# A hybrid encoder trunk on one core: the depthwise convolution's operations given a later rank in the scheduler's order

## The chip, the cores and the metric

The kernel runs on one core of a Trainium2 chip. The core has five engines with a queue each: PE (matrix products; the trace lists its weight loads as PEld), DVE (vector work), ACT (activations, scaled copies), POOL (elementwise work in SBUF) and SP (which issues the DMAs here). Each works through its own queue in the order in which it was written, and semaphores hold an instruction until what it reads is there and what it overwrites is free. The metric is the device time of one execution in microseconds; lower is better.

## The reference

Two batches, a prompt of 512 rows and a sample of 1024 rows, go through the same layer with the same weights (width 1024, float32). Cut to what matters:

```python
h = _rmsnorm(x, norm_attn_g)
z = h @ w_in                     # q 512 | k 128 | v 128 | ca 512 | cb 512
a_out = _window_attn(q, k, v, bias, band, attn_sink)        # |q - k| <= 128
c = ca * jax.nn.sigmoid(cb)
c = _dwconv(c, conv_dw_w, conv_dw_b)                        # 31 taps, 512 channels
c = jax.nn.silu(_layernorm(c, conv_ln_g, conv_ln_b))        # over the channels
x = x + jnp.concatenate([a_out, c], axis=-1) @ w_out
h = _rmsnorm(x, norm_ffn_g)
u = _dwconv(h @ w_up, ffn_dw_w, ffn_dw_b)                   # 3 taps
x = x + (jax.nn.silu(u[..., :D_FF]) * u[..., D_FF:]) @ w_down
y = _rmsnorm(x, norm_final_g)
```

The change concerns the order of the 31-tap convolution `c = _dwconv(...)` among all else.

## The kernel before, in words

Every matrix product is made of three products of split operands (a high part and a rest), 128x128 stationary against 512 columns. The work runs in stages that overlap:

1. The prompt's projection (lines 487 to 501): `order` lists 14 chunks of 128 columns of `w_in`: four pairs `cb`, `ca` first, then `k`, `v` and four `q`. `want_raw` loads a chunk, `want_w` splits it (`split`: a cast on ACT, L189, and a subtraction on POOL, L190), `step` multiplies it (`proj`, L296, L297, L299) into a PSUM bank and `evac` takes it out: for `cb` a tanh on ACT (L360), for `ca` the gating on DVE (L369) into a padded input `cp` whose borders POOL clears (L365, L366), for `q` L373 and L374. Beside it the sample's rows are normed (`norm_in_place`, L242 to L247, with `rstd_of` on POOL, L173 and L174) and turned (`transposed`: L255 on PE, L257 on ACT, L258 on DVE).
2. The sample's projection, and beside it the prompt's attention (`scores`: L560 on PE, L567 on DVE; `values`: L616 to L642), its layer norm (`conv_norm`, L669 to L695) and its output projection (`out_half`, L711 to L716).
3. The prompt's feed-forward, 22 steps (`ffn_step`, with L837 and L841), and beside it the sample's attention.
4. The sample's layer norms and output projection, and then its feed-forward by a Strassen-like scheme (from 790 us on), where PE's order is written by hand.

The convolution itself is `conv_items(g, c, cp)`, one generator for each batch `g` (0 the prompt, 1 the sample) and group `c` of 128 channels. It works in pieces of 512 columns, one in the prompt and two in the sample. In each piece DVE accumulates most of the 31 taps in one PSUM bank (L335, then L339 for each further tap); the last `NOFF[g]` taps (4 in the prompt, 7 in the sample) are products on ACT (L328, L331) which POOL sums up in `pacc` (L332); at the end DVE adds the two (L347), and SP stores the piece to `cvd` in DRAM (L349). `conv_norm` loads it from there (L669), turns it on PE (L675), takes mean and variance on DVE (L677, L678), `rstd_of` on POOL, scales on DVE (L681) and turns back (L687).

Which instruction is traced where is set by hand: `tick()` runs three times within a projection and after each step and takes as many steps of the convolution's generators from the queues `convs` (prompt) and `late` (sample) as a credit allows. `drain(convs)` in `conv_norm` and `drain(late)` before the sample's first `conv_norm` trace what is left.

The order in which an engine then gets its instructions is not the traced one. The program is traced whole; each instruction gets a rank, a counter (`tc.cur_priority`) that goes up by one with each instruction traced; then a scheduler walks through a simulated time and gives each engine that is free, of the instructions that are ready, the one with the lowest rank. An instruction is ready when its inputs are there and the buffer that it writes has been released. Buffers are single ones with a fixed name: the kernel's `Slots` deals them out while the program is traced (15 `q` of 4096 bytes, 61 `h` of 2048, 4 `c`, 2 `d`), so that a tile's next user is fixed in traced order, whatever the ranks. The eight PSUM banks are `a` (3), `u` (2), `b` (2) and `c` (1, the convolution's accumulator).

The central lines:

```python
acc = bank("conv")
nc.vector.tensor_scalar(acc[:], src(0), w(0), cvb[:, c:c + 1], op0=ALU.mult, op1=ALU.add)
yield cost
for t in range(1, CK - noff):
    nc.vector.scalar_tensor_tensor(acc[:], src(t), w(t), acc[:], op0=ALU.mult, op1=ALU.add)
    if t % 2 == 1 and k < noff:
        offload(k)
```

Of the kernel before, what the change touches and what calls it, by code (L numbers as in the profile page):

```python
# [54 lines left out]
VG = 3  # L55
NW = 36
KEEP = 3
U0 = 2


# [82 lines left out]
def tile_hybrid_encoder(ctx: ExitStack, tc: tile.TileContext, xs, rel_bias, norm_attn_g, w_in,  # L143
# [9 lines left out]

    sb = Slots(big, dict(q=(15, 4096), c=(4, 4224), h=(61, 2048), d=(2, 2176), s=(32, 64)), "q", KEEP)
    banks = Slots(lambda tag: ps[two_of[tag]], dict(a=(3, 2048), u=(2, 2048), b=(2, 2048), c=(1, 2048)))
# [5 lines left out]
    def bank(job):  # L161
        return banks.tile([NT], among=use[job])
# [111 lines left out]
    def tick():  # L274
        pace["credit"] += pace["conv"] if convs else pace["late"]
        queue = convs or (late if pace["late"] else convs)
        while queue and pace["credit"] > 0:
            pace["credit"] -= advance(queue)
        if not queue:
            pace["credit"] = 0.0  # L280
        pace["due"] += pace["rate"]
        while side and pace["due"] >= 1.0:
            advance(side)
            pace["due"] -= 1.0
        if not side:
            pace["due"] = 0.0
# [5 lines left out]
    def proj(out, w, h, late_lo=False):  # L292
        whi, wlo = w
        for kc in range(KC):
            hi, lo = h[kc]
            nc.tensor.matmul(out, whi[:, kc, :], hi[:], start=(kc == 0), stop=False)  # L296
            nc.tensor.matmul(out, whi[:, kc, :], lo[:], start=False, stop=False)  # L297
            if not late_lo:
                nc.tensor.matmul(out, wlo[:, kc, :], hi[:], start=False, stop=(kc == KC - 1))  # L299
            if kc % 2 == 1 and kc < KC - 1:  # L300
                tick()
        for kc in range(KC if late_lo else 0):
            nc.tensor.matmul(out, wlo[:, kc, :], h[kc][0][:], start=False, stop=(kc == KC - 1))
# [8 lines left out]

    convs, late = deque(), deque()

    def conv_items(g, c, cp):
        T = GR[g]["T"]
        w = lambda t: cvw[:, t * 4 + c:t * 4 + c + 1]
        cost = 0.13 + NT / 960.0
        noff = NOFF[g]
        off = list(range(CK - noff, CK))  # L320
        for n in range(T // NT):
            src = lambda t: cp[:, t + n * NT:t + (n + 1) * NT]
            pacc = sb.tile([NT])

            def offload(k):
                t = off[k]
                if k == 0:
                    nc.scalar.activation(pacc[:], src(t), AF.Identity, scale=w(t))  # L328
                else:
                    pr = sb.tile([NT])  # L330
                    nc.scalar.activation(pr[:], src(t), AF.Identity, scale=w(t))  # L331
                    nc.gpsimd.tensor_tensor(pacc[:], pacc[:], pr[:], op=ALU.add)  # L332
# [4 lines that stand above are left out]
            k = 0  # L337
# [4 lines that stand above are left out]
                    k += 1  # L342
                yield cost
            while k < noff:
                offload(k)
                k += 1
            nc.vector.tensor_tensor(pacc[:], acc[:], pacc[:], op=ALU.add)  # L347
            del acc
            nc.sync.dma_start(cvd[g][:, c, n * NT:(n + 1) * NT], pacc[:])  # L349
            yield cost  # L350

    tanh_t, cpads, kt, vt = {}, {}, {}, {}
# [77 lines left out]
    def step(i, nt):  # L430
        kind, c, col = order[i]
        pp = bank("step")
        proj(pp[:], ws[i], h1[nt], i < 2 and nt == 0)
        evac(kind, c, nt, pp[:])
        if kind == "ca" and nt != 1:
            g = 0 if nt == 0 else 1
            (convs, late)[g].append(conv_items(g, c, cpads.pop((g, c))))
        tick()

    want_raw(1)  # L440
# [47 lines left out]
    for i in range(npr):  # L488
        if i == 3:
            side.append(make_h1(1))  # L490
        if i == 5:
            xq[2] = [load_x(GR[1], 4 + i) for i in range(4)]
            side.append(make_h1(2))
        if i == 1:
            constants()
            bbd = bias_to_dram()
        want_raw(i + 2)
        want_w(i + 1)
        step(i, 0)
        ws.pop(i)  # L500
# [299 lines left out]
    for i in range(npr, nch):  # L800
        want_raw(i + 2)
        want_w(i + 1)
        if i == nch - 1:
            for half in range(2):
                want_up_raw(0, half)
        for nt in range(1, 3):
            step(i, nt)
        ws.pop(i)
# [91 lines left out]
    def sample():  # L900
        sink_columns()
        yield from attention(8, 24)
        kt.clear(), vt.clear(), qt.clear(), bias.clear(), score_rows.clear()
        use.update(norm="a")
        pace.update(rate=RN)
        for m in range(16 + WOA):
            if m in (10, 12):
                load_cat(m // 2 - 1)
            if m < 16:
                load_wo(m // 2, m % 2)  # L910
            if m >= WOA:
                split_wo((m - WOA) // 2, m % 2, m % 4 < DW2)
                yield 0.0
        drain(late)
        for m in range(NE):
            yield from conv_norm(4 + m)

    pace.update(rate=RD, late=CD)
    for k in range(NJ):
        if k == U0:  # L920
            side.append(sample())
# [721 lines left out]
```

## Time and profile before

| | us |
|---|---|
| median of 3 runs | 1563.84 (1559.77 to 1566.2) |
| the profiled execution, its time | 1558.91 |
| the profiled execution, its span | 1557.1 |
| PE busy | 1506.9 |
| DVE busy | 1126.2 |
| ACT busy | 795.4 |
| POOL busy | 708.9 |

The profile is of one execution. A line of its timeline gives the start, the duration, engine and line of the kernel, the operation, the tile written and those read, and in brackets how long the engine stood idle before, and what ended that. A line of the waits gives who waited for whom, the sum, the number of times and the longest. A stage's row gives its length and, for each engine, the busy time and the number of instructions in it; PEclk is the share of PE's full clock that was granted. Idle time of an engine that isn't the bottleneck costs nothing.

### The profile page before, as it was taken

Reading aid. Unit: us, or ns where it says so; the run is one execution under the profiler, and the core shown is the slowest. Engines: PE = TensorE matmul, PEld = TensorE weight load, DVE = VectorE, ACT = ScalarE, POOL = GpSimd, SP = SyncE. Lnnn points to the kernel's source line nnn. Section 1 sums busy time; section 2 is a strip of 40 time slices with the busy share of each in tenths; the row PEclk is TensorE's granted clock in tenths of the full one; section 3 lists DMA queues with packets and bytes.
Section 4 is the critical chain, followed back from the end, with each engine's and each line's share of the span. In section 5 each row is a group of like instructions: output and inputs, shape, how many; then the busy total and the mean of one; then the engine's idle time right before and its main releaser. Section 6 shows DMA issues by size and latency. Waiting matters only on the chain. (4 is left out here: it accounts for less than half of the span.)

```text
span 1557.1 us, 20112 instructions
## 1 busy us (share of the span) xinstructions
PE 1506.9 (97%) x6843; PEld 1229.4 (79%) x6843; DVE 1126.2 (72%) x1604; ACT 795.4 (51%) x1404; POOL 708.9 (46%) x566
## 2 busy tenths in 40 slices
PE   8899998999999999899999999999999999999997
PEld 6787787787888888777777888888888788888885
DVE  7999767857788785344868777777776845568883
ACT  4634654335787786633454444455545543444254
POOL 7652344226666776947433455555554000003355
PEclk9999999999999999999999999999999999999999
DMA  7582334447343346779332233333331582356644
GB/s 230 156 212 81 107 100 124 129 142 217 112 132 129 118 129 181 242 238 298 114 93 76 92 104 104 105 104 102 102 115 64 200 284 82 105 165 230 221 135 162
DMA packets 228780, 227.17 MB, mean 146 GB/s; under 512 B 13268, under 2 KB 168348, under 8 KB 228549
## 3 DMA queue, kind: packets, MB, share of 16 engines
q1 hardware_dynamic: 228677, 225.88, 45.8%
q8 instruction: 54, 0.88, 0.2%
q14 instruction: 49, 0.40, 0.1%
HBM read 164.74 MB, written 62.14 MB: 146 GB/s over the span
## 5 line engine op out<-in xcount | busy, mean ns | idle before, releaser
L190 POOL TENSOR_TENSOR q<-q,q 128x1024 fp32r<-128x1024 f32 x72 | 173.4, 2415 | 93.4 <-ACT q L189 34.4
L940 POOL TENSOR_TENSOR q<-q,q 128x512 fp32r<-128x512 f32 x101 | 140.0, 1391 | 164.0 <-ACT q L1050 151.7
L940 DVE TENSOR_TENSOR h<-h,h 128x512 fp32r<-128x512 f32 (+2 forms) x202 | 153.9, 794 | 65.2 <-ACT h L944 25.3
L1398 PE MATMUL w<-h,h 128*128 128x512 f32 x462 | 181.4, 393 | 1.4 <-DVE q L1185 1.4
L1399 PE MATMUL w<-h,h 128*128 128x512 f32 x462 | 181.5, 393 | 0.0
L1400 PE MATMUL w<-h,h 128*128 128x512 f32 x462 | 181.1, 392 | 0.0
L1064 PE MATMUL w<-h,q 128*128 128x512 f32 x448 | 176.5, 394 | 1.0 <-ACT h L1147 0.6
L1066 PE MATMUL w<-h,q 128*128 128x512 f32 x448 | 175.5, 392 | 1.0 <-POOL q L940 1.0
L1065 PE MATMUL w<-h,q 128*128 128x512 f32 x426 | 166.4, 391 | 0.0
L296 PE MATMUL u<-h,q 128*128 128x512 f32 x400 | 161.0, 403 | 5.4 <-DVE h L837 4.1
L297 PE MATMUL u<-h,q 128*128 128x512 f32 x400 | 158.6, 397 | 0.0
L299 PE MATMUL u<-h,q 128*128 128x512 f32 x384 | 151.8, 395 | 2.7 <-POOL q L190 2.7
L937 POOL TENSOR_TENSOR q<-q,q 128x1024 f32<-128x1024 f32 x12 | 32.4, 2707 | 236.6 <-DVE q L937 220.0
L339 DVE SCALAR_TENSOR_TENSOR c<-c,cvw,c 128x512 f32<-128x512 f32 x184 | 138.0, 750 | 2.9
L944 ACT CAST h<-h 128x512 fp32r<-128x512 f32 x120 | 71.9, 619 | 93.2 <-DVE h L940 41.9
L296 PE MATMUL b<-h,q 128*128 128x512 f32 x256 | 102.7, 401 | 3.3 <-DVE d L369 2.2
L1398 PEld LDWEIGHTS w<-h,h 128*128 128x128 f32 x462 | 86.8, 188 | 21.6 <-ACT h L944 1.8
L1400 PEld LDWEIGHTS w<-h,h 128*128 128x128 f32 x462 | 86.7, 188 | 19.7
L1399 PEld LDWEIGHTS w<-h,h 128*128 128x128 f32 x462 | 86.8, 188 | 19.5
L837 DVE SCALAR_TENSOR_TENSOR h<-u,fw,h 128x511 f32<-128x511 f32 x88 | 65.5, 744 | 49.8 <-ACT h L841 49.0
L299 PE MATMUL b<-h,q 128*128 128x512 f32 x256 | 101.4, 396 | 0.0
L297 PE MATMUL b<-h,q 128*128 128x512 f32 x256 | 101.1, 395 | 0.0
(417 smaller groups left out, 3670.4 us busy)
## 6 DMA issues: line engine op xcount, KB each, us to landing
q<-in_w_up SPq DMA_DIRECT2D x88, 512.0 KB
ga<-q SPq DMA_DIRECT2D x64, 256.0 KB
h<-ga SPq DMA_DIRECT2D x57, 256.0 KB
q<-in_w_in SPq DMA_DIRECT2D x28, 512.0 KB
h<-in_w_down SPq DMA_DIRECT2D x52, 256.0 KB
q<-in_x_sample SPq DMA_DIRECT2D x15, 512.0 KB
h<-qsd SPq DMA_DIRECT2D x24, 256.0 KB
x1d<-q SPq DMA_DIRECT2D x11, 512.0 KB
```

The costliest lines, as they stand in the source:

```text
L190: (nc.vector if dve else nc.gpsimd).tensor_tensor(lo[:], raw[:], hi[:].bitcast(F32), op=ALU.subtract)
L296: nc.tensor.matmul(out, whi[:, kc, :], hi[:], start=(kc == 0), stop=False)
L297: nc.tensor.matmul(out, whi[:, kc, :], lo[:], start=False, stop=False)
L299: nc.tensor.matmul(out, wlo[:, kc, :], hi[:], start=False, stop=(kc == KC - 1))
L339: nc.vector.scalar_tensor_tensor(acc[:], src(t), w(t), acc[:], op0=ALU.mult, op1=ALU.add)
L940: (eng or nc.vector).tensor_tensor(out, a, b, op=ALU.subtract)
L1064: nc.tensor.matmul(out, whi[:, s], hi[:], start=(start and c == 0), stop=False, **go)
L1065: nc.tensor.matmul(out, whi[:, s], lo[:], start=False, stop=False, **go)
L1066: nc.tensor.matmul(out, wlo[:, s], hi[:], start=False, stop=(stop and c == 3), **go)
L1398: nc.tensor.matmul(out, sh[:, c], th[:], start=(p == 0), stop=False)
L1399: nc.tensor.matmul(out, sh[:, c], tl[:], start=False, stop=False)
L1400: nc.tensor.matmul(out, sl[:, c], th[:], start=False, stop=(p == NPAIR - 1))
```

## The change

The generator of each convolution is wrapped in another one, `behind`. Around each step it raises the rank counter by `n` and takes it back afterwards, so that whatever the step traces has a rank that is `n` higher: 200 in the prompt, 1500 in the sample. What is traced, where it is traced, the buffers and the paces stay as they are.

```diff
+BACK = (200, 1500)
...
     convs, late = deque(), deque()
+
+    def behind(gen, n):
+
+        while True:
+            tc.cur_priority += n
+            try:
+                cost = next(gen)
+            except StopIteration:
+                return
+            finally:
+                tc.cur_priority -= n
+            yield cost
...
         if kind == "ca" and nt != 1:
             g = 0 if nt == 0 else 1
-            (convs, late)[g].append(conv_items(g, c, cpads.pop((g, c))))
+            (convs, late)[g].append(behind(conv_items(g, c, cpads.pop((g, c))), BACK[g]))
```

## The prediction

> **What bounds the kernel now.** I read the page's busy line first, then the busy time by stage, then the waits of PE in the first stages, then the timeline around each wait.
>
> ```profile
> span 1557.1 us, 20112 instructions
> DVE  7999767857788785344868777777776845568883
> 40.00:181.00 141.00, 130.33 (x625) 106.07 (x624) 126.86 (x222) 74.62 (x147) 64.97 (x46) 0.99 0.50 139
> 181.00:260.00 79.00, 78.09 (x375) 63.90 (x374) 60.38 (x113) 43.55 (x93) 33.01 (x24) 1.00 0.44 118
> 260.00:280.00 20.00, 13.03 (x54) 10.47 (x53) 9.20 (x15) 8.55 (x17) 9.06 (x10) 0.74 0.40 125
> 280.00:640.00 360.00, 358.05 (x1698) 296.67 (x1698) 274.11 (x501) 236.09 (x436) 210.91 (x137) 1.00 0.48 147
> 640.00:800.00 160.00, 150.37 (x701) 121.26 (x700) 87.09 (x126) 61.74 (x117) 92.29 (x107) 0.98 0.61 200
> ```
>
> The columns of a stage are its length, then the busy time and count of PE, PEld, DVE, ACT and POOL, and PE's granted clock. PE carries the kernel: from 280 to 640 us it is idle for 360.00 - 358.05 = 1.95 us. It loses time in two places where the convolution also runs: 141.00 - 130.33 = 10.67 us between 40 and 181, and 6.97 us in the twenty microseconds from 260. In the first, DVE is itself busy 126.86 of 141 us (90%), and most of that is the prompt's convolution:
>
> ```profile
> 40.00:181.00 141.00, 78.29 (x104) 0.99 0.50 139
> 181.00:587.00 406.00, 138.00 (x184) 0.99 0.44 132
> ```
>
> This is the same view for line 339 alone, the taps on DVE: 78.29 of 126.86 us, 62%, in the prompt's stretch; in the sample's, 138.00 us spread over 406. So the question is how often a tap stands in front of something that PE waits for, and what a later convolution holds up in turn.
>
> **The change part by part.** Nothing is removed or added: the same instructions, tiles and DMAs, and the same buffers given out in the same order. What moves is the place of the convolution's instructions: in each of the prompt's four pieces 28 on DVE, 4 products on ACT, 3 sums on POOL and a store on SP, 144 in all, and in each of the sample's eight 25, 7, 6 and 1, 312 in all, within the order that the planner writes for each engine. By the counts of the stages above, PE, DVE, ACT and POOL together take 625+222+147+46 = 1040 instructions in 141 us, and 1698+501+436+137 = 2772 in 360: 7.4 and 7.7 per us. A rank 200 later is therefore about 27 us (estimate), one 1500 later about 195 us: in the prompt a step back, in the sample the end of every queue.
>
> *DVE in the prompt's stretch (gain).* The waits of PE from 40 to 181, but for one on ACT and one on a DMA:
>
> ```profile
> PE b L296 <- DVE d L369: 2.2, 1, 2.2
> PE u L616 <- DVE s L567: 2.0, 2, 1.1
> PE a L560 <- DVE s L567: 1.7, 1, 1.7
> PE u L299 <- POOL q L190: 1.2, 1, 1.2
> ...
> PE a L255 <- DVE h L258: 0.8, 1, 0.8
> PE a L631 <- DVE q L619: 0.6, 1, 0.6
> PE a L616 <- DVE s L583: 0.6, 1, 0.6
> ...
> PE b L296 <- DVE h L384: 0.4, 1, 0.4
> ```
>
> DVE ends 2.2+2.0+1.7+0.8+0.6+0.6+0.4 = 8.3 us of them. The two longest single ones in the timeline:
>
> ```profile
> 51.06 0.75 DVE L339 SCALAR_TENSOR_TENSOR c<-d,cvw,c 128x512 f32<-128x512 f32 x1
> 51.72 0.68 DVE L369 SCALAR_TENSOR_TENSOR d<-h,b 128x512 f32<-128x512 f32 x1
> 52.45 0.50 PE L296 MATMUL b<-h,q 128*128 128x512 f32 x1 [2.19 <-DVE d L369]
> ...
> 119.33 2.34 DVE L339 SCALAR_TENSOR_TENSOR c<-q,cvw,c 128x512 f32<-128x512 f32 x3
> 121.58 0.48 DVE L567 CUSTOM_DVE_ANT_0 h<-u,h,nsink 128x256 f32<-128x256 f32 x1
> 123.49 0.48 PE L560 MATMUL a<-h,h 128*128 128x256 f32 x2 [1.65 <-DVE s L567]
> ```
>
> A tap starts right before the evacuation (L369) that PE needs, and three run before the scores' evacuation (L567). A tap that ranks behind lets these go first, up to the one that is already running. The gain lies between 0 and 8.3 us; I take the taps' share of DVE's work, 62%, as the chance that the thing in front was a tap: **5.1 us**.
>
> *POOL around 265 (gain).*
>
> ```profile
> 268.60 1.26 POOL L332 TENSOR_TENSOR q<-q,q 128x512 f32<-128x512 f32 x1 [3.29 <-ACT q L331]
> 269.95 0.19 POOL L173 TENSOR_SCALAR s<-s 128x1 f32<-128x1 f32 x1
> 271.69 1.12 PE L687 MATMUL u<-ident,q 128*128 128x128 f32 x4 [4.03 <-DVE q L681]
> 276.61 1.09 PE L687 MATMUL u<-ident,h 128*128 128x128 f32 x4 [2.94 <-DVE h L681]
> ```
>
> PE stands 4.03 and 2.94 us for the prompt's last two layer norms. A sum of the sample's convolution (L332) runs 1.26 us on POOL just ahead of the first norm's variance (L173). Its rank falls by 1500, but POOL was idle when it became ready, and the planner doesn't hold a free engine back; so 0 to 1.3 us of the wait itself. The clock granted in that stage is 0.74: 13.03 us of work lose about 3.4 us by it, 10.4 with the idle time. I take the 1.3 and its share of the lost clock, 1.3/6.97 of 3.4: **1.9 us**; the bounds are minus and plus 10.4, since the order of this stage is written anew.
>
> [...]
>
> *The sample's convolution (nothing).* From 280 to 640 only 1.95 us of PE can be won. What a late end would cost depends on its first reader:
>
> ```profile
> 182.91 0.32 SPq L349 DMA_DIRECT2D cvd<-h  x1
> 194.24 0.58 SPq L669 DMA_DIRECT2D h<-cvd  x1
> ...
> 587.55 0.42 SPq L349 DMA_DIRECT2D cvd<-h  x1
> 663.22 0.57 SPq L669 DMA_DIRECT2D h<-cvd  x1
> 181.00:587.00 406.00, 396.17 (x1864) 326.79 (x1863) 315.01 (x568) 248.27 (x468) 216.13 (x148) 0.99 0.44 132
> ```
>
> The last piece of the sample is stored (L349) at 587.55 and read first (L669) at 663.22: 75.7 us of cover. All other DVE work in the 406 us is 315.01 - 138.00 = 177 us, 44%, so a tap that always goes last meets a free engine more than half the time: 0.75 us stretch to about 0.75/0.56 = 1.3, and a piece of 23 taps from 17 to 31 us, where the eight pieces now take 406/8 = 51 us each. The lag doesn't add up from piece to piece; I put the end 10 to 30 us later, inside the cover: 0. If the cover were gone, each microsecond past it would be one on PE's path. The prompt has less: stored at 182.91, read at 194.24, 11.3 us. Its taps can only lose what other work gains in front of them, 5 us by the term above; again 0, with up to 27 - 11.3 = 15.7 us of lateness if it lost all of its 200 ranks, which PE would fill with the sample's projections (the stage 181 to 260 has 78.09 of 79 us busy).
>
> *The buffers (nothing, with a bad upper end).* Each convolution tile is a single buffer whose next user was fixed in program order and waits for it, whatever its rank.
>
> ```profile
> 76.29 0.11 POOL L365 MEMSET d<- 128x15 f32 x1 [4.04 <-DVE c L339]
> 76.42 4.77 POOL L190 TENSOR_TENSOR q<-q,q 128x1024 fp32r<-128x1024 f32 x2
> ```
>
> The fourth prompt channel's input reuses the first one's buffer: POOL stood 4.04 us until the first channel's last tap, with two weight splits (L190) behind it. Postponing taps makes this later. PE has waited only 1.2 us for a split here (the L299 row above), so I take 0; the upper end is the first rival.
>
> *A rule against the change.* A tap accumulates in PSUM and keeps its time, while the norm's scaling (L247), which now goes first, does not:
>
> ```profile
> L339 DVE SCALAR_TENSOR_TENSOR c<-d,cvw,c x78: 740/756/757, 40.9 to 165.6; 128x512 f32<-128x512 f32 x78
> 50.39 0.75 DVE L247 TENSOR_SCALAR q<-q,s 128x1024 f32<-128x1024 f32 x1 [0.44 <-POOL s L174]
> 59.96 2.38 POOL L190 TENSOR_TENSOR q<-q,q 128x1024 fp32r<-128x1024 f32 x1
> 60.48 2.40 DVE L247 TENSOR_SCALAR q<-q,s 128x1024 f32<-128x1024 f32 x1
> ```
>
> L247 takes 0.75 us alone and 2.40 beside a split on POOL. The number of such meetings may go either way by a few, at 1.65 us of DVE each; I take none. [...]
>
> *Sum.* 5.1 + 1.9 = 7.0 us less. The profiled execution has a span of 1557.1 us and a time of 1558.91, 0.3% under the median of 1563.84. 1558.91 - 7.0 = 1551.9; against the median, times 1563.84/1558.91, **1557 us**.
>
> **The rivals.**
>
> *Slots in place of ranks (slower).* The convolution's tiles come free later, and what was given the same buffers waits: the memset above with the splits behind it, then in the sample the products and partial sums that sit in the half buffers of the weights (the q of the L332 row at 268.60 is such a half). For it: the 4.04 us on POOL, and that PE already waits 1.2 us for a split, so that the splits have no lead to spare there. Against: the planner sees these waits and fills an idle DVE with taps. Price: half of the 27 us of rank in the prompt, 13.5, and as much again from 181 to 280, where the weights are still split: 1558.91 + 27 = 1585.9, against the median about 1591; half of that, 1577, if only one of them bites. It decides from the point where the last tap of a piece moves by more than the lead of the split behind it.
>
> *The sample's convolution ends after its reader (slower).* If it really lost its 195 us of rank, it would end 195 - 75.7 = 119 us past the need, and PE would have little else: 1560 + 60 or more. Against: DVE's 56% of free time. Unlikely.
>
> *Nothing moves.* The taps already are what fills DVE: the planner gave evacuations with an earlier rank the way, and pieces end when the offloaded sums end, not the taps. A rank changes only ties; the step back isn't "behind all else" where nothing else is ready. 1558 to 1566 us.
>
> *The gain is eaten on DVE.* Four scalings (L247) or norms meet a split that they missed before: 4 x 1.65 = 6.6 us on an engine that is 90% busy, which leaves 0.4 of the 7.0: 1563 us. For it: the 2.40 above; against: as many may part.
>
> *Both holes close (much faster).* All of DVE's waits and the whole stage at 260: 8.3 + 10.4 = 18.7 us, 1540.2, against the median 1545.
>
> **How the numbers follow.** I tell no change from one within 0.5%, 7.8 us: faster is under 1556.0, slower over 1571.7. The forecast has a chance of 0.50 with its own range of 1549 to 1564, so near the bound that it gives 0.27 to faster and 0.23 to the same. Slots: 0.27, of it 0.25 slower. The late sample: 0.05, slower. Nothing moves: 0.05, the same. The gain eaten: 0.04, of it 0.03 the same, 0.01 slower. Both holes: 0.09, faster. Together faster 0.36, same 0.33, slower 0.31. The range leaves out the late sample and the tail of the slots above, and below it allows a little more than both holes: 1539 to 1592.
>
> **What would show it.** In the changed profile PE's waits between 40 and 181 that DVE ends fall from 8.3 to about 3 us; L369 and L567 no longer start right behind a tap. The stage from 260 (wherever the last norms then lie) keeps most of its hole. The last store of the sample's convolution lies between 597 and 618 us and no read of it waits; from 280 to 640 PE is idle 2 us or so. I am wrong if new waits of PE on POOL's L190 or on evacuations held up by a buffer appear between 60 and 280 (the slots), if PE waits for L669 after 640 (the late sample), or if the taps stand where they stood (nothing moves).

## The result: no change, and the profile after

The changed kernel takes 1562.26 us in the median of 12 runs (1558.83 to 1567.08); the kernel before, beside it, 1563.74 (1559.77 to 1571.06). The ratio is 0.9992, with a 95% interval of 0.9977 to 1.0007: no change. The forecast was 1557, 7 us less.

Lines of the changed kernel stand 3 higher than before up to line 314 and 15 higher behind it: the taps are L354, the gating L384, the scores' evacuation L582, the sum on POOL L347, the store L364 and its reader L684. In the profiled execution (span 1559.5 us, 1561.29 with what lies around it) the busy time by stage, with the columns as before:

```profile
40.00:181.00 141.00, 129.69 (x621) 105.35 (x620) 126.49 (x220) 74.10 (x146) 63.63 (x46) 0.99 0.50 140
181.00:260.00 79.00, 77.97 (x376) 63.94 (x375) 60.24 (x114) 43.49 (x94) 33.15 (x25) 1.00 0.43 116
260.00:280.00 20.00, 12.04 (x54) 9.40 (x53) 9.82 (x16) 7.72 (x14) 7.78 (x9) 0.82 0.43 131
280.00:640.00 360.00, 358.50 (x1699) 297.80 (x1698) 274.22 (x501) 236.73 (x439) 211.35 (x138) 1.00 0.47 147
```

and the same for the taps alone:

```profile
40.00:181.00 141.00, 78.27 (x104) 0.99 0.50 140
```

In each of these stages every engine has the busy time that it had, within 1.4 us, and the prompt's 104 taps lie in the stretch where they lay. PE's waits that DVE ends, from 40 to 181 us:

```profile
PE u L631 <- DVE s L582: 2.0, 2, 1.1
PE b L299 <- DVE d L384: 1.9, 1, 1.9
PE a L575 <- DVE s L582: 1.8, 1, 1.8
```

With three shorter ones (0.8, 0.6 and 0.6) they sum to 7.7 us where they were 8.3, and are the same waits but for one of 0.4. The timeline shows why:

```profile
50.13 0.75 DVE L250 TENSOR_SCALAR q<-q,s 128x1024 f32<-128x1024 f32 x1
50.80 0.75 DVE L354 SCALAR_TENSOR_TENSOR c<-d,cvw,c 128x512 f32<-128x512 f32 x1
51.45 0.68 DVE L384 SCALAR_TENSOR_TENSOR d<-h,b 128x512 f32<-128x512 f32 x1
52.19 0.50 PE L299 MATMUL b<-h,q 128*128 128x512 f32 x1 [1.87 <-DVE d L384]
...
113.13 8.66 DVE L354 SCALAR_TENSOR_TENSOR c<-q,cvw,c 128x512 f32<-128x512 f32 x11
121.69 0.48 DVE L582 CUSTOM_DVE_ANT_0 h<-u,h,nsink 128x256 f32<-128x256 f32 x1
120.83 0.49 PE L575 MATMUL u<-h,h 128*128 128x256 f32 x2 [1.14 <-DMA h<-qsd]
...
269.20 1.26 POOL L347 TENSOR_TENSOR q<-q,q 128x512 f32<-128x512 f32 x1 [3.27 <-ACT q L346]
270.55 0.19 POOL L176 TENSOR_SCALAR s<-s 128x1 f32<-128x1 f32 x1
272.30 0.66 PE L702 MATMUL u<-ident,q 128*128 128x128 f32 x4 [4.03 <-DVE q L696]
```

The tap still stands ahead of the gating, the taps ahead of the scores' evacuation, the sum ahead of the norm's variance. It isn't a new order that happens to cost the same. The two compiled programs hold the same instructions in the same order on all five engines, although 456 instructions (4 x 36 and 8 x 39) carry a rank that is 200 or 1500 higher. How many instructions of each engine's compiled program (those for semaphores and control left out) are not the ones that stand at the same place before, by the step that the ranks take:

```
step (prompt, sample)       PE   DVE   ACT  POOL   SP
(200, 1500)                  0     0     0     0    0
(100000, 100000)             0     0     0     0    0
(-20, 0) and (0, -20)        0     0     0     0    0
(-200, -1500)              910   359   181    72   89
```

So a step back, as far as 100000, picks nothing else, and a far step ahead does. In the planner's simulated time no convolution instruction went first by its rank: where another instruction of its engine was ready beside it, that one had the lower rank already, and else the convolution had the engine to itself. The change asked for what was already so.

### The profile page after: what moved, and what is told of

Its sections match the earlier page's. It is cut to its first block, busy times and chain, and to the rows that moved or that the text cites. A ratio compares the mean times of both kernels' runs of the same rounds, so it can differ in the third digit from the quotient of the medians.

```text
span 1559.5 us, 20112 instructions
## 1 busy us (share of the span) xinstructions
PE 1505.8 (97%) x6843; PEld 1228.9 (79%) x6843; DVE 1126.9 (72%) x1604; ACT 795.2 (51%) x1404; POOL 709.7 (46%) x566
## 5 line engine op out<-in xcount | busy, mean ns | idle before, releaser
L955 DVE TENSOR_TENSOR h<-h,h 128x512 fp32r<-128x512 f32 (+2 forms) x202 | 158.4, 817 | 66.2 <-ACT h L959 26.1
L302 PE MATMUL u<-h,q 128*128 128x512 f32 x384 | 152.2, 396 | 2.7 <-POOL q L193 2.7
L354 DVE SCALAR_TENSOR_TENSOR c<-c,cvw,c 128x512 f32<-128x512 f32 x184 | 137.9, 750 | 2.9
L299 PE MATMUL b<-h,q 128*128 128x512 f32 x256 | 102.3, 400 | 2.7 <-DVE d L384 1.9
L1079 PEld LDWEIGHTS w<-h,q 128*128 128x128 f32 x448 | 84.2, 188 | 22.5 <-ACT w L1171 2.1
L302 PE MATMUL b<-h,q 128*128 128x512 f32 x256 | 101.3, 396 | 0.0
```

What stands on the lines that cost most here:

```text
L955: (eng or nc.vector).tensor_tensor(out, a, b, op=ALU.subtract)
L1079: nc.tensor.matmul(out, whi[:, s], hi[:], start=(start and c == 0), stop=False, **go)
```

## The experiments

The expectations call the parts of the prediction steps: A is DVE in the prompt's stretch, B is POOL around 265, C is the sample's convolution. Each ratio is to the kernel before, run on the same chip; the interval is 95%.

| run | median, us | ratio | interval |
|---|---|---|---|
| ranks 0 and 0 | 1565.16 | 1.0014 | 1.0001 to 1.0027 |
| ranks in front | 1568.77 | 1.0032 | 1.0020 to 1.0043 |
| prompt's taps ordered behind | 1576.93 | 1.0092 | 1.0066 to 1.0117 |
| sample's taps ordered behind | 1564.63 | 1.0010 | 0.9996 to 1.0025 |
| few taps, prompt, pace shifted | 1577.65 | 1.0088 | 1.0073 to 1.0104 |
| few taps, sample, pace shifted | 1570.16 | 1.0054 | 1.0037 to 1.0071 |
| two prompt pieces ordered behind | 1565.87 | 1.0017 | 1.0006 to 1.0029 |
| sample's sums on POOL ordered behind | 1565.44 | 1.0009 | 0.9992 to 1.0026 |
| few taps, prompt, pace kept | 1557.95 | 0.9967 | 0.9956 to 0.9979 |
| few taps, sample, pace kept | 1567.14 | 1.0027 | 1.0013 to 1.0040 |
| pieces traced whole, ranks 0 and 0 | 1703.38 | 1.0893 | 1.0866 to 1.0920 |
| pieces traced whole, ranks 200 and 1500 | 1710.08 | 1.0938 | 1.0913 to 1.0963 |

### Ranks of 0, and ranks in front

```diff
-BACK = (200, 1500)
+BACK = (0, 0)
```

> The ranks are set to 0 and 0 in the changed kernel, everything else stays. Theory 1 (nothing moves: the step back picks no other instruction on any engine, so before, after and this are one program): 1.000 of the kernel before, give or take 0.003, and in the trace the taps stand where they stand in after, with a tap or three right ahead of the same two evacuations. Theory 2 (the ranks did move taps, and two effects cancelled): the engines' busy time by stage and the waits of PE from 40 to 181 us differ between this run and after by more than a microsecond in some stage, while the sum stays.

The ratio is 1.0014. This is the program of before with the wrapper around the generators, and its order is that of before on every engine. Its interval begins just above 1, so one part in a thousand is what two copies of one program can differ by here. In its trace the sum on POOL starts at 269.14 us (269.20 after, 268.60 before): theory 1. One wait of PE, on ACT (L633), is 2.4 us here and 1.2 after, and the waits that DVE ends from 40 to 181 us sum to 7.4 (7.7 after, 8.3 before): so much do single executions of one program differ.

```diff
-BACK = (200, 1500)
+BACK = (-200, -1500)
```

> The convolution ranked in front instead of behind: minus 200 and minus 1500. Theory 1 (a convolution instruction already went only where nothing else was ready, so only the other direction can change a pick): the order moves now; evacuations of the prompt's stretch come later by a tap now and then, PE's waits on DVE between 40 and 181 us rise from 8.3 to 10 to 20 us, and the time rises by 2 to 15 us, ratio 1.001 to 1.010; the sample's part costs nothing, since PE stays idle about 2 us from 280 to 640. Rival (ranks have no hold on these instructions in either direction): 1.000 and the same waits. Rival (slots: an early end of the convolution frees its buffers sooner): 5 to 15 us faster, with the waits on the splits gone.

It is 5 us slower (0.32%): theory 1 in sign and size, not in place. PE's waits on DVE fell, to 4.5 us; what rose is a wait of the prompt's first scores, and the first reader of the prompt's convolution came later (202.52 us, 194.75 after). In its waits from 40 to 181:

```profile
PE u L575 <- DMA h<-qsd: 3.4, 1, 3.4
```

The wait on `qsd` was 1.1 us. Ranks do have a hold on these instructions, in the other direction.

### The step back made to hold

Each step's instructions on DVE are queued behind the last DVE instruction of other work that was traced before it, whatever the planner's times say.

```diff
-    def behind(gen, n):
+    def behind(gen, after):
...
+                last = next(i for i in reversed(nc.cur_bb.bb.instructions)
+                            if i.engine == mybir.EngineType.DVE and i.name not in steps_of)
...
+                    with tc.issue_after(last):
+                        cost = next(gen)
```

First on the prompt alone:

```diff
-BACK = (200, 1500)
+BACK = (True, False)
```

> Each step of the prompt's convolution has its DVE instructions ordered behind the last DVE instruction of other work that the program wrote before it, which is the step back made to hold whatever the plan's times say. If step A of the prediction is right in its price (a tap ahead of an evacuation costs PE 5.1 us, and a tap put behind lets it go first): PE's waits on DVE from 40 to 181 us fall from 8.3 to about 3 us, 3 to 5 us faster, ratio 0.997 to 0.998. If the taps were what filled DVE's free time and their place cost PE little: DVE stands idle in front of an ordered tap, the prompt's last store moves from 182.9 to beyond 200 us, and the time is the same or up to 15 us longer, ratio 1.000 to 1.010. If slots decide: new waits of PE on POOL's weight splits of 5 us or more between 60 and 280 us.

Here lines stand 24 higher than before (taps L363, gating L393). DVE and PE in its timeline:

```profile
49.98 0.75 DVE L250 TENSOR_SCALAR q<-q,s 128x1024 f32<-128x1024 f32 x1
50.65 0.68 DVE L393 SCALAR_TENSOR_TENSOR d<-h,b 128x512 f32<-128x512 f32 x1
51.25 0.75 DVE L363 SCALAR_TENSOR_TENSOR c<-d,cvw,c 128x512 f32<-128x512 f32 x1
...
51.39 0.50 PE L299 MATMUL b<-h,q 128*128 128x512 f32 x1 [1.06 <-DVE d L393]
```

The swap that the prediction wanted has happened: the gating goes ahead of the tap, and PE goes on at 51.39 us in place of 52.19, 0.8 us sooner. Of that, 0.15 lies ahead of the tap, since the norm's scaling (L250) starts at 49.98 in place of 50.13; the tap itself is worth 0.65 us of a wait of 1.87. The rest is the scaling ahead of both and the gating's own time. Against that stands PE's new idle time from 181 to 260, where it is busy 66.52 us in place of 77.97. Its longest waits there, and then, from the timeline of SP, the prompt's last store and the first reader:

```profile
PE u L699 <- DMA h<-cvd: 4.6, 1, 4.6
PE a L711 <- DVE h L705: 3.7, 1, 3.7
```

```profile
223.41 0.34 SPq L373 DMA_DIRECT2D cvd<-h  x1
225.78 0.57 SPq L693 DMA_DIRECT2D h<-cvd  x1
```

The prompt's last store has moved from 183.42 to 223.41 us, 29 us past the time at which it was read before (194.75), and the norm, and with it PE, waits. That fits the 11.3 us of cover that the prediction named for a late prompt.

Then on two of its pieces:

```diff
-            (convs, late)[g].append(behind(conv_items(g, c, cpads.pop((g, c))), BACK[g]))
+            (convs, late)[g].append(behind(conv_items(g, c, cpads.pop((g, c))), BACK[g] and c < 2))
```

> The order of the run with the ordered prompt for the first two of the prompt's four pieces alone, so that the last piece ends in time for its reader. It separates what an ordered tap brings from what the late end costs. Theory (a tap in front costs at most its own 0.75 us): the gating that stood behind a tap at 51.5 us goes first again, PE's wait for it is 1.0 to 1.2 us instead of 1.9; the prompt's last store stays within 5 us of 183.4; the time is the same, ratio 0.998 to 1.001. Rival (step A's price, half of it in these two pieces): 2 us or more faster, ratio 0.9985 or less with its interval below 1. Rival (the gaps on DVE cost by themselves, not the late end): 5 us or more slower.

The prompt's last store is at 186.75 us and the first reader at 202.65; the swap at the gating is there too (L393 at 50.75). PE's wait for it is 2.26 us, and not the expected 1.0 to 1.2, because PE comes to it sooner (its last turn ahead of it starts at 48.62 us, 49.72 after); the products go on at 51.48, 0.7 us sooner than after. The time is 0.17% above before, close to what a second copy of the program showed: a little above the theory's range, with an interval that reaches into it. The rival with 2 us of gain is out, and so is the one with 5 us of loss. A wait that is larger than this gain comes later, in the timelines of ACT, DVE and PE:

```profile
111.47 0.69 DVE L371 TENSOR_TENSOR h<-c,h 128x512 f32<-128x512 f32 x1
...
116.95 0.60 ACT L397 ACTIVATE h<-a 128x512 fp32r<-128x512 f32 x1 [3.13 <-DMA cvd<-h]
117.66 0.69 DVE L398 SCALAR_TENSOR_TENSOR h<-a,h 128x512 fp32r<-128x512 f32 x1 [2.27 <-ACT h L397]
...
124.90 0.76 PE L584 MATMUL u<-h,h 128*128 128x256 f32 x2 [5.19 <-DMA h<-qsd]
```

The second piece ends with L371 and is stored at 113.44 us (105.56 after). The copy of a query chunk (L397) waits for that store, because it was dealt the buffer that the store reads. The rest of the chunk (L398) follows at 117.66 (112.53 after), its way through `qsd` is later, and the scores wait 5.19 us, where they waited 1.14. It is the mechanism of the rival "slots in place of ranks", seen at one place and with a price of 4 us.

And on the sample alone:

```diff
-BACK = (200, 1500)
+BACK = (False, True)
```

> The same order for the sample's eight pieces alone. By step C of the prediction (75.7 us of cover before the first reader, PE idle 1.95 us from 280 to 640): the last store of the sample's convolution moves from 587.6 to between 597 and 660 us and the time stays, ratio 0.998 to 1.002. Rival (the late sample): the store passes 663 us, PE waits for its reader, and each microsecond past it costs one. Rival (slots): the products and sums that sit in the weights' half buffers hold up splits, and PE waits on POOL by 5 us or more between 181 and 640.

The time is that of before. The last store moves from 588.42 to 621.99 us, inside the bounds, with 48 us left to its first reader on SP:

```profile
621.99 0.52 SPq L373 DMA_DIRECT2D cvd<-h  x1
670.13 0.57 SPq L693 DMA_DIRECT2D h<-cvd  x1
```

### The sums on POOL ordered behind

The same with the last POOL instruction, for the sample; DVE, ACT and SP get no such order.

```diff
-                            if i.engine == mybir.EngineType.DVE and i.name not in steps_of)
+                            if i.engine == mybir.EngineType.Pool and i.name not in steps_of)
```

> Each step of the sample's convolution has its sums on POOL ordered behind the last POOL instruction of other work that the program wrote before it; DVE, ACT and SP as in before. It is step B of the prediction by itself. If B holds: the sum that runs just ahead of the first norm's variance near 270 us goes behind it, PE's first wait there falls from 4.0 to about 2.7 us, and the time falls by 1 to 3 us, ratio 0.998 to 0.9995. If the sum was there because POOL was free until the variance came: it moves, the wait shrinks by 0 to 0.6 us, and the time stays. Rival (slots): the sums' tiles sit in the weights' half buffers, PE waits on weight splits by 3 us or more between 181 and 640, and the time rises.

POOL and PE around the prompt's last two norms, with L699 their first turn and L711 the second:

```profile
267.09 0.19 POOL L176 TENSOR_SCALAR s<-s 128x1 f32<-128x1 f32 x1 [2.60 <-DVE s L702]
...
267.90 2.61 POOL L356 TENSOR_TENSOR q<-q,q 128x512 f32<-128x512 f32 x2
...
264.64 0.60 PE L699 MATMUL a<-ident,q 128*128 128x128 f32 x4
265.00 0.47 PE L302 MATMUL b<-h,q 128*128 128x512 f32 x1
...
268.83 0.66 PE L711 MATMUL u<-ident,q 128*128 128x128 f32 x4 [1.97 <-DVE q L705]
272.79 1.09 PE L711 MATMUL u<-ident,h 128*128 128x128 f32 x4 [2.86 <-DVE h L705]
...
382.32 0.47 PE L299 MATMUL u<-h,q 128*128 128x512 f32 x1 [2.85 <-DVE h L861]
```

The variance goes ahead of the sum, and PE's two waits are 1.97 and 2.86 us in place of 4.03 and 2.97. But little of this is the sum. From the first turn to the second it takes 268.83 - 264.64 = 4.19 us here and 272.30 - 267.67 = 4.63 after (its first turn, L690, starts at 267.67): 0.44 us. The rest of the shorter wait comes from products (L302 and those up to 266.86) that the new order puts between the turns. And at 382 us PE stands 2.85 us for a step of the feed-forward on DVE, a wait that the changed kernel doesn't have there: its PE is busy 358.50 us from 280 to 640, this one's 355.83. What was won at 270 was lost at 382, and the time is that of before: the second expectation (0 to 0.6 us off the wait) holds, and step B's price doesn't.

### Most of the taps left out

```diff
-            for t in range(1, CK - noff):
+            for t in range(1, (7 if g == 0 else CK - noff)):
```

> In each of the prompt's four pieces only six further taps stay on DVE; the other 20 are left out of the sum, so the output differs. It is the ceiling of what any place of the prompt's taps could bring, since 80 of the 104 are gone (60 us of DVE's work between 40 and 181 us). If the price of step A holds (62 per cent of DVE's 8.3 us of waits are taps in front): PE's waits on DVE from 40 to 181 us fall by 5 us or more, to about 3. If most of each wait is the chain itself (products, evacuation, next products), as the run with the ordered prompt read it at the gating (0.8 us gained of 1.9): the waits fall by 2 to 3 us, to about 5, and the stage from 260 stays as it was. The time: 2 to 7 us less, ratio 0.9955 to 0.999.

> The same in the sample's eight pieces: six further taps stay, 17 are left out (136 in all, 102 us of DVE's work between 181 and 590 us). By step C (PE idle 1.95 us from 280 to 640) the taps' place is worth nothing there: ratio 0.997 to 1.002, most of a gain, if any, in the stage from 260. Rival (the sample's taps hold up PE where the profile puts the wait on something else): 5 us or more faster, with PE's busy share from 280 to 640 unchanged and the gain after 640.

Both are misses: 14 and 8 us slower with 80 and 136 taps fewer. A step that is gone also leaves the pace, so the later pieces are traced sooner, and buffers are dealt in another order. To tell the two apart, the generator keeps its steps and only the tap is left out:

```diff
-                nc.vector.scalar_tensor_tensor(acc[:], src(t), w(t), acc[:], op0=ALU.mult, op1=ALU.add)
+                if g != 0 or t < 7: nc.vector.scalar_tensor_tensor(acc[:], src(t), w(t), acc[:], op0=ALU.mult, op1=ALU.add)
```

> The run with six further taps in each of the prompt's pieces again, but a step of the generator that leaves out its tap still counts in the pace, so that all else is traced where it was; the same 80 taps are left out of the sum. The first run of this kind mixed two things: fewer taps, and a sample's convolution traced earlier (its first store at 181.9 instead of 234 us). If the taps in front of evacuations cost PE what step A says: waits on DVE from 40 to 181 us fall by 5 us or more from 7.7, and the time by 4 us or more, ratio 0.9975 or less. If a tap in front costs its own 0.75 us at the few places where one stands: the waits fall by 1 to 3 us, and the time by 0 to 3 us, ratio 0.998 to 1.000. If the 14 us lost by the first run of this kind came from the missing taps themselves and not from the tracing: 5 us or more slower.

It is 5.2 us faster (0.33% of 1563.34). So where the steps are traced is worth some 19 us (1.0088 against 0.9967), more than the taps themselves. Its stage from 40 to 181, and PE's waits there that DVE ends:

```profile
40.00:181.00 141.00, 132.71 (x633) 109.20 (x633) 73.49 (x145) 76.37 (x152) 63.77 (x46) 0.98 0.50 144
```

```profile
PE a L258 <- DVE h L261: 3.4, 1, 3.4
...
PE b L299 <- DVE d L384: 1.3, 1, 1.3
PE a L646 <- DVE d L634: 1.1, 2, 0.9
PE u L631 <- DVE s L582: 0.4, 1, 0.4
```

DVE is busy 73.49 of 141 us in place of 126.49, and DVE ends 6.2 us of waits in place of 7.7. That falls in the second expectation (1 to 3 us), while the time falls in the first (4 us or more). The 6.2 hold a wait that grew: 3.4 us for an evacuation of the sample's turned rows (L261), 0.8 after, which starts at 58.01 us here (54.03 after). The other waits fall from 6.9 to 2.8 us. At the gating, with no tap on DVE from 46 to 55 us, 1.3 of the 1.87 us remain: there the wait is mostly the chain, and the tap a part of it. By 181 us PE has worked 132.71 us in place of 129.69, and the prompt's last two norms then hold it up for 2.2 and 3.4 us in place of 4.0 and 3.0. The run takes taps away, which no rank does, so 5.2 us is a ceiling for the place of these 80.

> The same for the sample's eight pieces, with the pace kept; 136 taps are left out of the sum. By step C: from 280 to 640 PE stays idle 1 to 3 us, ratio 0.997 to 1.001. If the 7 us that the first run of this kind lost (PE waits of 8.2 us on ACT between 280 and 640) came from the tracing, they are gone here; if they came from DVE's missing work, they stay, ratio 1.004 or more.

By 663.00 us, where the first reader of the sample's convolution is issued, this run is level with before (663.22): the 102 us of DVE's work were worth nothing up to there. It loses its 4 us (0.27%, twice what two copies of one program showed) behind that point, among the last norms at first: PE's wait for reads of `cvd` is 4.0 us from 640 to 800 (1.6 after). Why the order planned there is worse stays open.

### Pieces traced whole

Here a step back has something to act on: each piece is traced in one go behind its gating.

```diff
+            drain((convs, late)[g])
```

> Each piece of the convolution is traced in one go, right behind the gating that completes its input, in place of the pace's step by step; ranks not stepped back (0 and 0). By the theory that the pace had already put each step behind what it competes with, this takes that away: taps and products stand in front of evacuations and norms traced later, PE's waits from 40 to 260 us rise by 5 us or more, 5 to 25 us slower, ratio 1.003 to 1.016. If the traced place does not matter: 0.998 to 1.002.

> The same with the change's ranks, 200 and 1500. It is the control for the rank: here a step back has something to act on. By the theory above the order differs from the run without a step back, and a part of its loss comes back: 2 us or more faster than that run. If the rank is without effect on the time even where it changes the order: the same within 2 us.

The first is 140 us slower than before, far more than I expected; the second is some 7 us slower still, although the step back changes the order here (81 instructions on DVE and 398 on PE stand at another place). One wait shows why it doesn't help. DVE, PE and SP without the step back, then with it (lines 15 or 16 higher than before):

```profile
141.22 11.83 DVE L354 SCALAR_TENSOR_TENSOR c<-d,cvw,c 128x512 f32<-128x512 f32 x15
...
153.88 0.32 SPq L364 DMA_DIRECT2D cvd<-h  x1
...
154.74 1.55 DVE L354 SCALAR_TENSOR_TENSOR c<-c,cvw,c 128x512 f32<-128x512 f32 x2
156.23 0.69 DVE L389 SCALAR_TENSOR_TENSOR h<-b,h 128x512 fp32r<-128x512 f32 x1
156.98 0.80 PE L299 MATMUL b<-h,q 128*128 128x512 f32 x1 [16.20 <-DVE h L389]
```

```profile
156.21 0.32 SPq L364 DMA_DIRECT2D cvd<-h  x1
...
158.57 0.69 DVE L389 SCALAR_TENSOR_TENSOR h<-b,h 128x512 fp32r<-128x512 f32 x1
159.31 0.79 PE L299 MATMUL b<-h,q 128*128 128x512 f32 x1 [16.21 <-DVE h L389]
```

Seventeen taps and the end of a piece stand ahead of a query's evacuation, and PE waits 16.2 us for it, with the ranks of 200 and 1500 as without; in a program with 100000 for both the same instructions still stand there. The reason is a buffer. In all three compiled programs the evacuation writes into the `h` buffer (number 33) that holds the sum of the prompt's fourth piece, and it waits for the store of that sum, which is issued at 153.88 us. Until the piece has ended and been stored the evacuation isn't ready, and no rank can bring it forward. It is the rival "slots in place of ranks" again, this time brought about by the place of tracing. Where the rest of the 140 us comes from (PE's longest waits are of 19.9, 23.5 and 17.6 us, for attention and weights) I didn't follow: it stays open.

## Why the prediction was wrong, step by step

**What bounds the kernel.** This held: PE carries it, and the two stages with idle PE are where they were.

**DVE in the prompt's stretch (5.1 us): the step that failed.** The prediction put it: "A tap that ranks behind lets these go first." It failed twice. First, a tap in front on the chip was read as a tap that had won by its rank. The order is written in the planner's time beforehand, and there no tap had ever won: the step back changed no pick, and even 100000 changes none. The gating shows the difference: on the chip it was ready by 50.65 us, where the ordered run starts it, and yet a rank of 100000 doesn't get it ahead of the tap, so in the planner's time it wasn't ready when the tap was picked. The 27 and 195 us that the prediction made of the ranks fell with this: the prompt's last store is at 183.42 us (182.91 before), the sample's at 588.42 (587.55). Second, the size. All of a wait was put to the tap with a chance of 62%, where one tap in front holds up an evacuation that is ready by its own 0.75 us at most. Ordered ahead of its tap, the gating brought 0.65 us of 1.87. At the scores not even that: of the eleven taps from 113.13 each takes 0.79, so the last starts at about 121.0, ahead of the end of the product (120.83 + 0.49 = 121.32) that the evacuation reads. Nothing that was ready was passed over, and the tap's end at 121.79, some 0.5 us behind the product's, is at most what it cost. Leaving out 80 taps took 5.2 us off the time, but that run also takes 53 us of work from DVE, which no later place does: the forecast's 5.1 asked for the whole of this ceiling, that the two figures agree is chance, and the two orders that held brought no gain in time.

**POOL around 265 (1.9 us).** The same failure: the sum stayed ahead of the variance. With the order forced, the time from turn to turn shortened by 0.44 us, not 1.3, and a new wait of 2.85 us at 382 took more than that back.

**The sample's convolution (nothing).** Right, though nothing moved: with its taps ordered behind, it ended at 621.99 us and cost nothing. The estimate of 10 to 30 us of lateness became 33.6 by the stronger order.

**The prompt's cover of 11.3 us.** The change didn't touch it; the ordered prompt ended 40 us later and lost 14 us, so this was the number that mattered for a step back that holds.

**The buffers (nothing) and the rival of the slots.** No buffer changed its time. Where the order was forced, one did: a store 7.9 us late held a query's copy 3.13 us and the scores 5.19 in place of 1.14. The mechanism was right, at 4 us and not at 13.5 to 27. With the pieces traced whole, the same mechanism made PE wait 16.2 us.

**The scaling beside a split (nothing).** The scaling at 60.22 us takes 2.40 us beside a split, as it did before (60.48, 2.40): no meeting changed, as nothing moved, and no run tested it.

**Nothing moves (given 0.05).** This is what happened, for the reason that its first sentences give. The prediction had both halves of the argument, that taps fill DVE's free time and that a rank changes only ties, and gave more weight to the timeline of the chip, which can't tell a lost tie from an instruction that wasn't yet ready in the plan.

## What to carry to other kernels

A rank decides only among instructions that are ready at the same moment of the planner's time, with the buffer that they write free, so first see whether the order on any engine differs at all; an operation that stands in front on the chip is no proof that it won. Price an operation in front by its own length, not by the wait behind it, and look for what the wait holds besides: here the tap was 0.65 of 1.87 us. A filler that is really put behind pays with its end, through the reader of its result and through the buffers that it holds.

## What the runs showed of the hardware

With the sums ordered behind on POOL, PE stood for 1.97 and 2.86 us at the prompt's last two norms (4.03 and 2.97 in the changed kernel), with 1.1 us of turns between, and the granted clock fell all the same: from 260 to 280 its mean is 0.75, where the changed kernel has 0.82. The busy time by stage around it, PE first and the granted clock third from the end:

```profile
268.00:271.00 3.00, 1.09 (x8) 0.86 (x8) 1.66 (x3) 1.47 (x5) 2.46 (x3) 0.85 0.00 0
271.00:274.00 3.00, 1.09 (x4) 0.72 (x4) 1.75 (x2) 1.76 (x5) 2.84 (x4) 0.50 0.34 87
...
277.00:280.00 3.00, 3.00 (x8) 2.32 (x8) 1.81 (x3) 1.74 (x4) 2.74 (x2) 0.50 0.95 260
280.00:284.00 4.00, 4.00 (x18) 3.22 (x18) 3.88 (x6) 2.88 (x5) 0.15 (x1) 0.96 0.70 180
```

From 265 to 268 us the clock was 1.00. The 0.85 from 268 to 271, if it is made of 1.00 ahead of the fall and the next row's 0.50 behind it, puts the fall at about 270.1 (an estimate), 0.2 us into the second wait, which begins at 269.93. A product of 512 columns starts every 0.43 us up to 280.18 and every 0.23 from 280.48 on, so the clock is back at about 280.2, 4.9 us after PE's last idle time ends (275.32). In the changed kernel the pace changes in the same way at 282.80, 3.6 us after that point (279.22). What makes the clock fall, and what sets the time of its return, no run here shows.
